# The up projection of a conv FFN with its weights stationary: transposes and copies of u left out

## The chip, the cores and the metric

The program runs on one core of one Trainium2 chip, in one launch. The metric is device microseconds of an execution; the time before is the median of three runs. One more execution was profiled, and the rows below come from that one.

## What is computed

Two transformer blocks, one after the other, on 256 tokens of width 2048, in float32. The change lies in the feed-forward part of the first block:

```
def conv_ffn(h, w_up, w_conv, b_conv, w_down):
    u = h @ w_up                                  # 256 x 2048 by 2048 x 11264
    up = jnp.pad(u, ((0, 0), (CONV_W - 1, 0), (0, 0)))
    conv = b_conv
    for j in range(CONV_W):                       # CONV_W = 3, over the tokens
        conv = conv + w_conv[j] * up[:, j:j + S]
    gate, val = jnp.split(conv, 2, axis=-1)
    return (jax.nn.silu(gate) * val) @ w_down     # 256 x 5632 by 5632 x 2048
```

`h` is the normalised input, with a shift and a scale that come from `c`. The convolution runs along the tokens, with weights of its own for each of the 11264 features.

## The kernel before, in words

Every large product is made of three: each float32 operand is split into a high and a low part (type fp32r), and high x high, high x low and low x high are summed in PSUM. A **unit** is one block of 256 x 512 weights (512 KB): a DMA on SyncE's queue brings it into a `raw` tile (6 buffers), ScalarE casts the high part into an `hl` tile (line 157, 5 buffers), VectorE subtracts for the low part (line 79), and TensorE makes 12 matmuls of it. In between stand jobs that `pump` puts in (`vec_unit`, lines 170 to 175): each loads 512 KB of the modulation weights `w_ada` or `w_mod` into a `raw` tile of the same six and lets VectorE reduce it against `c` in one instruction (L175).

`gemm_gen` (lines 366 to 401) has the activations stationary: `lhsT` is a 128 x 128 piece of `h` (128 features by 128 tokens), the weights move with 512 columns, and the sum stands in PSUM with tokens on the partitions. `up_half` copies it to `u` with ScalarE (L1012), or adds it to `u` with VectorE (L79). The convolution needs the features on the partitions and the tokens along the row, so `conv_half` transposes `u` with TensorE in 8 pieces of 128 x 128 (L1025), into two PSUM tiles `tp`. Then come, for each of 4 groups of 128 features, one ScalarE instruction with bias and the last tap (L1029) and two VectorE instructions for the other taps (L1031, L1033). `glu` multiplies silu(gate) with val and splits the product into `gThi` and `gTlo`.

A **half** is 512 features of gate or of val; a pair `j` of 11 is one half of each. The first four pairs are made in two passes: the first pass (`NH`) makes k = 0 to 7 of their 8 halves (4 units each) while the rest of `h` is still waiting for its scale; the second makes k = 8 to 15 (4 units each). The other 7 pairs have 8 units in each half. The pairs come in four rounds (0 to 2, 3 to 5, 6 to 8, 9 and 10), and each round is followed by its part of the down projection: 4 columns blocks `c`, each of 6 units (4 in the last round), in the order of the pairs; so the units of the round's last pair stand at the end of each block.

Four PSUM tiles `mm` of 2 KB a partition go round; each half and each column block takes two. Program order is not the order on the engines: a scheduler orders the instructions of each engine when the program is built, and each engine then runs its own list in that order. In the list of an engine a waiting instruction holds back all behind it.

Of the kernel before, what the change touches and what calls it, by code (L numbers as in the profile page):

```python
# [13 lines left out]
AF = mybir.ActivationFunctionType  # L14
# [7 lines left out]
KT = 2  # L22
# [7 lines left out]
def block_pair_kernel(ctx: ExitStack, tc: tile.TileContext, T: dict, out: bass.AP):  # L30
# [32 lines left out]
    def ps_mm(name="mm"):  # L63
        n_s4[0] += 1
        return psp.tile([128, 512], F32, name=f"{name}_{n_s4[0]}", tag="mm", bufs=4)
# [98 lines left out]
    def pump(n):  # L164
        for _ in range(n):
            if not jobs:
                return
            jobs.popleft()()
# [101 lines left out]
    def load_split(blk, n, big=False):  # L270

        raw = raw_tile()
        nc.sync.dma_start(raw[:, :KT * n], blk)
        rv = raw[:, :KT * n].rearrange("p (k n) -> p k n", k=KT)
        if big:
            hl = [s4([128, KT, 512], F32R, name="hl")[:, :, :n] for _ in range(2)]
        else:
            n_s4[0] += 1
            t = sp.tile([128, 2, KT, 512], F32R, name=f"hl_{n_s4[0]}", tag="hl", bufs=NHL)
            hl = [t[:, b, :, :n] for b in range(2)]  # L280
        split(hl[0], hl[1], rv)
        return hl
# [719 lines left out]
    gT = {}  # L1002
    us = {}

    def up_half(j, half, k, nk, rate, head=0):
        if (j, half) not in us:
            us[j, half] = s4([128, 2, 512], name="u")
        u = us[j, half]

        def ev(t, p):  # L1010
            if k == 0:
                SC.copy(u[:, t, :], p)  # L1012
            else:
                tt(u[:, t, :], u[:, t, :], p, OP.add)
        gemm(stF, T["w_up"][half * 11 + j], k, nk, ev, rate=rate, head=head)

    def conv_half(j, half):
        u = us.pop((j, half))
        cv = s4([128, 4, 256], name="cv")
        for b in range(2):  # L1020
            p = ps_tp([128, 2, 256])
            for i in range(2):
                for t in range(2):
                    f = b * 2 + i
                    PE.transpose(p[:, i, t * 128:(t + 1) * 128], u[:, t, f * 128:(f + 1) * 128], ident)  # L1025
            for i in range(2):
                f = b * 2 + i
                fi = half * 44 + j * 4 + f
                SC.activation(cv[:, f, :], p[:, i, :], AF.Identity, bias=wcv[:, 3, fi:fi + 1],  # L1029
                              scale=wcv[:, 2, fi:fi + 1])  # L1030
                V.scalar_tensor_tensor(cv[:, f, 1:], p[:, i, :255], wcv[:, 1, fi:fi + 1], cv[:, f, 1:],  # L1031
                                       op0=OP.mult, op1=OP.add)
                V.scalar_tensor_tensor(cv[:, f, 2:], p[:, i, :254], wcv[:, 0, fi:fi + 1], cv[:, f, 2:],  # L1033
                                       op0=OP.mult, op1=OP.add)
        return cv

    def glu(j, cg, cv):
        SC.activation(cg, cg, AF.Silu)
        tt(cv, cg, cv, OP.mult)
        hi = s4([128, 4, 256], F32R, name="gThi")  # L1040
        lo = s4([128, 4, 256], F32R, name="gTlo")
        split(hi, lo, cv)
        gT[j] = (hi, lo)

    def ffn_pair(j, rate):
        k, nk = (8, 8) if j < NH else (0, 16)
        up_half(j, 0, k, nk, rate)
        cg = conv_half(j, 0)
        up_half(j, 1, k, nk, rate)
        glu(j, cg, conv_half(j, 1))  # L1050


    for j in range(NH):
        for half in range(2):
            up_half(j, half, 0, 8, RH, head=HEAD if (j, half) == (0, 0) else 0)
    pump(1000)
    norm_to_pairs(hF, range(4, 8), x1T, rB, A2, SH2)
    job_row("w_ada", 0, 80, COL_BGTF, gtF)
# [247 lines left out]
```

## Time and profile before

| what | us |
|---|---|
| median of 3 runs | 1740.43 |
| lowest, highest | 1739.60, 1742.21 |
| the profiled execution | 1743.09 |
| its span in the trace | 1741.3 |
| TensorE matmul busy | 1692.9 (97%) |
| TensorE weight load busy | 1385.5 (80%) |
| VectorE busy | 1369.1 (79%) |
| ScalarE busy | 910.8 (52%) |

The span is from the first to the last instruction of the program; the 1.8 us around it are start and end. TensorE has two rows: PE is the matmuls, PEld the loads of the stationary operand, which run beside them. Matmuls overlap and their ends are modelled, so 97% busy does not tell how fast they follow each other; that is read from their starts.

### The profile page before, as it was taken

To read this page: it belongs to the slowest core of one execution; us is meant where nothing else is said; L and a number is where in the kernel's file an instruction comes from. 1 tells how busy PE (TensorE), PEld (TensorE's weight loads), DVE (VectorE), ACT (ScalarE), POOL (GpSimd) and SP (SyncE) were. 2 spreads that over 40 slices of the span, in tenths; PEclk is the share of its full clock that TensorE was granted. 3 is DMA by queue.
4 is the path that set the end of the run, shared out by engine and by line. 5 is a ranking of instruction groups with operands and counts; after the bars stand their busy time and mean duration, and the time that the engine had idled before them with its cause. 6 is when DMAs were issued, how large, how long until landed. Compare 5 with 4: busy or idle time off the path is not lost.

```text
span 1741.3 us, 22010 instructions
## 1 busy us (share of the span) xinstructions
PE 1692.9 (97%) x7786; PEld 1385.5 (80%) x7786; DVE 1369.1 (79%) x2079; ACT 910.8 (52%) x1283; POOL 4.2 (0%) x15
## 2 busy tenths in 40 slices
PE   8899999999999989999999999999999999999997
PEld 6688888878778868788888788887888777888886
DVE  8899999998978767599677676777877777766765
ACT  4644354767854456555455544555345565454443
POOL 0000000000000000000000000000000000000000
PEclk9999999999999999999999999999999999999999
DMA  8999988588868868677877787777777748778762
GB/s 324 342 333 324 339 324 278 191 295 295 277 224 323 287 206 313 214 242 238 296 247 251 232 268 261 260 245 261 272 255 252 248 160 269 255 254 277 238 201 94
DMA packets 127495, 455.59 MB, mean 262 GB/s; under 512 B 14357, under 2 KB 15893, under 8 KB 127385
## 3 DMA queue, kind: packets, MB, share of 16 engines
q1 hardware_dynamic: 127384, 454.19, 77.0%
q8 instruction: 61, 1.00, 0.2%
q14 instruction: 50, 0.40, 0.1%
HBM read 452.04 MB, written 2.10 MB: 261 GB/s over the span
## 4 chain that ended last, share of the span: by engine, by line
PE 59%; DMA 18%; DVE 14%; issue 5%; ACT 3%; SPq 0%; DVEq 0%; ACTq 0%
PE mm L378 51%; DMA raw<-in_w_mod 13%; DVE hl L79 5%; DMA raw<-in_w_ada 4%; DVE raw L175 3%; PE keep L378 2%; ACT hl L157 1%; PE mm L1171 1%; DVE cv L1031 1%; PE tp L1025 1%; DVE score L599 1%; DVE cv L1033 0%; DVE pacc L79 0%; PE tp L922 0%; DMA cst<-in_cst 0%
## 5 line engine op out<-in xcount | busy, mean ns | idle before, releaser
L157 ACT CAST hl<-raw 128x1024 fp32r<-128x1024 f32 (+2 forms) x564 | 586.6, 1046 | 584.5 <-PE mm L378 432.0
L79 DVE TENSOR_TENSOR hl<-raw,hl 128x1024 fp32r<-128x1024 f32 (+2 forms) x564 | 675.7, 1212 | 141.5 <-ACT hl L157 140.8
L378 PE MATMUL mm<-hl,hN 128*128 128x512 f32 x2880 | 676.4, 394 | 6.6 <-DVE hN L79 2.4
L378 PEld LDWEIGHTS mm<-hl,hN 128*128 128x128 f32 x2880 | 540.8, 190 | 121.3 <-DVE hN L79 4.0
L175 DVE SCALAR_TENSOR_TENSOR raw<-raw,cB 128x1024 f32<-128x1024 f32 x288 | 350.5, 1220 | 184.7 <-DMA raw<-in_w_mod 139.9
L378 PE MATMUL mm<-hl,hT 128*128 128x512 f32 (+1 forms) x1248 | 290.9, 392 | 8.0 <-ACT hT L157 3.3
L378 PEld LDWEIGHTS mm<-hl,hT 128*128 128x128 f32 x1248 | 234.2, 190 | 56.5 <-ACT hl L157 4.1
L378 PE MATMUL mm<-hl,gThi 128*128 128x512 f32 x704 | 219.9, 395 | 6.2 <-DVE hl L79 3.4
L378 PEld LDWEIGHTS mm<-hl,gThi 128*128 128x128 f32 x704 | 132.9, 190 | 35.9 <-DVE hl L79 5.0
L378 PE MATMUL mm<-hl,gTlo 128*128 128x512 f32 x352 | 137.8, 395 | 0.0
L378 PE MATMUL mm<-hl,pair 128*128 128x512 f32 x384 | 89.5, 392 | 0.0
L378 PE MATMUL mm<-hl,zT 128*128 128x512 f32 x384 | 87.5, 389 | 0.0
L378 PEld LDWEIGHTS mm<-hl,zT 128*128 128x128 f32 x384 | 71.9, 188 | 14.8
L378 PEld LDWEIGHTS mm<-hl,pair 128*128 128x128 f32 x384 | 71.5, 188 | 14.6
L378 PEld LDWEIGHTS mm<-hl,gTlo 128*128 128x128 f32 x352 | 66.9, 190 | 13.8 <-DVE gTlo L79 0.2
L1029 ACT ACTIVATE cv<-tp,wcv 128x256 f32<-128x256 f32 x88 | 44.9, 562 | 47.9 <-DVE cv L1033 39.4
L79 DVE TENSOR_TENSOR pacc<-pacc,mm 128x512 f32<-128x512 f32 (+1 forms) x78 | 52.2, 671 | 6.8 <-PE mm L378 6.3
L378 PE MATMUL mm<-hl,oaT 128*128 128x512 f32 x192 | 48.0, 399 | 0.0
L378 PE MATMUL mm<-hl,obT 128*128 128x512 f32 x192 | 47.1, 397 | 0.6 <-DVE obT L79 0.6
L378 PE MATMUL keep<-hl,hT 128*128 128x512 f32 x192 | 45.7, 395 | 0.8 <-DVE hl L79 0.8
L378 PEld LDWEIGHTS keep<-hl,hT 128*128 128x128 f32 x192 | 36.5, 191 | 9.0 <-DVE hl L79 1.6
L378 PEld LDWEIGHTS mm<-hl,obT 128*128 128x128 f32 x192 | 35.1, 188 | 8.0 <-DVE obT L79 1.0
(331 smaller groups left out, 1191.1 us busy)
## 6 DMA issues: line engine op xcount, KB each, us to landing
raw<-in_w_ada SPq DMA_DIRECT2D x192, 512.0 KB, 4.8
raw<-in_w_up SPq DMA_DIRECT2D x176, 512.0 KB, 4.6
raw<-in_w_in SPq DMA_DIRECT2D x112, 512.0 KB, 5.1
raw<-in_w_mod SPq DMA_DIRECT2D x96, 512.0 KB, 4.5
raw<-in_w_down SPq DMA_DIRECT2D x88, 512.0 KB, 4.6
raw<-in_pool_w_in SPq DMA_DIRECT2D x64, 512.0 KB, 4.5
raw<-in_w_o SPq DMA_DIRECT2D x32, 512.0 KB, 4.9
raw<-in_pool_w_out SPq DMA_DIRECT2D x32, 512.0 KB, 4.3
```

Source lines behind the costliest of these rows:

```text
L79: return V.tensor_tensor(o, a, b, op=op)
L157: SC.copy(hi, src)
L175: V.scalar_tensor_tensor(raw, raw, 1.0, cact[cv][h], op0=OP.mult, op1=OP.mult, accum_out=acc)
L378: PE.matmul(ps[t][:, :n], lhsT=st(k0 + k, t, a), rhs=hl[b][:, i, :], start=(part[0] and k == 0 and x == 0), stop=(part[1] and k == nk - 1 ...
L599: V.scalar_tensor_tensor(score, r[:, i, :], w, score, op0=OP.mult, op1=OP.add)
L1025: PE.transpose(p[:, i, t * 128:(t + 1) * 128], u[:, t, f * 128:(f + 1) * 128], ident)
L1029: SC.activation(cv[:, f, :], p[:, i, :], AF.Identity, bias=wcv[:, 3, fi:fi + 1], scale=wcv[:, 2, fi:fi + 1])
L1031: V.scalar_tensor_tensor(cv[:, f, 1:], p[:, i, :255], wcv[:, 1, fi:fi + 1], cv[:, f, 1:], op0=OP.mult, op1=OP.add)
L1171: PE.matmul(pv[:, q, :], lhsT=hls[k // 2][wa][:, k % 2, f * 128:(f + 1) * 128], rhs=pooled[i][xb][:, k, :], start=(k == 0 and x == 0), sto ...
```

## The change

All halves but the first half of the first pair (in both of its passes) are now made by `up_feat`: for each unit the weights are stationary in 4 pieces of 128 features, and the 256 tokens of `h` move, so that PSUM has the features on the partitions. A unit is 24 matmuls of 256 columns in place of 12 of 512. The four PSUM rows of a half (two tiles, two rows of 256 in each) are held from its first matmul to its last tap. `taps` is the old code of the convolution in a function of its own; it reads the sums from PSUM, or, for the pairs in two passes, from `uT`, to which the second pass is added (`tt`). The copies of `u`, the transposes and the tiles `u` of these halves are gone.

```
+    def up_feat(j, half, k, nk, rate):
+        W = T["w_up"][half * 11 + j]
+        ps = [ps_mm().rearrange("p (q t) -> p q t", q=2) for _ in range(2)]
+        nu = nk // KT
+        for u in range(nu):
+            hl = load_split(W[k // KT + u], 512)
+            for f in range(4):
+                for i in range(KT):
+                    for x, (a, b) in enumerate(((0, 0), (1, 0), (0, 1))):
+                        PE.matmul(ps[f // 2][:, f % 2, :], lhsT=hl[a][:, i, f * 128:(f + 1) * 128],
+                                  rhs=hF[k // 2 + u][:, b, i, :], start=(u == 0 and i == 0 and x == 0 and f % 2 == 0),
+                                  stop=(u == nu - 1 and i == KT - 1 and x == 2), skip_group_check=True)
+            credit[0] += rate
+            while credit[0] >= 1.0:
+                pump(1)
+                credit[0] -= 1.0
+        return ps
+
+    def up_first(j, half, rate):
+        ps = up_feat(j, half, 0, 8, rate)
+        u = us[j, half] = s4([128, 4, 256], name="uT")
+        for b in range(2):
+            SC.copy(u[:, 2 * b:2 * b + 2, :], ps[b])
+
+    def taps(j, half, cv, b, p):
+        for i in range(2):
+            f = b * 2 + i
+            fi = half * 44 + j * 4 + f
+            SC.activation(cv[:, f, :], p[:, i, :], AF.Identity, bias=wcv[:, 3, fi:fi + 1],
+                          scale=wcv[:, 2, fi:fi + 1])
+            V.scalar_tensor_tensor(cv[:, f, 1:], p[:, i, :255], wcv[:, 1, fi:fi + 1], cv[:, f, 1:],
+                                   op0=OP.mult, op1=OP.add)
+            V.scalar_tensor_tensor(cv[:, f, 2:], p[:, i, :254], wcv[:, 0, fi:fi + 1], cv[:, f, 2:],
+                                   op0=OP.mult, op1=OP.add)
+
+    def up_conv(j, half, rate):
+        u = us.pop((j, half), None)
+        ps = up_feat(j, half, 0 if u is None else 8, 16 if u is None else 8, rate)
+        cv = s4([128, 4, 256], name="cv")
+        for b in range(2):
+            p = ps[b]
+            if u is not None:
+                p = u[:, 2 * b:2 * b + 2, :]
+                tt(p, p, ps[b], OP.add)
+            taps(j, half, cv, b, p)
+        return cv
...
     def ffn_pair(j, rate):
-        k, nk = (8, 8) if j < NH else (0, 16)
-        up_half(j, 0, k, nk, rate)
-        cg = conv_half(j, 0)
-        up_half(j, 1, k, nk, rate)
-        glu(j, cg, conv_half(j, 1))
+        if j == 0:
+            up_half(j, 0, 8, 8, rate)
+            cg = conv_half(j, 0)
+        else:
+            cg = up_conv(j, 0, rate)
+        glu(j, cg, up_conv(j, 1, rate))
...
-            up_half(j, half, 0, 8, RH, head=HEAD if (j, half) == (0, 0) else 0)
+            if (j, half) == (0, 0):
+                up_half(j, half, 0, 8, RH, head=HEAD)
+            else:
+                up_first(j, half, RH)
```

How the order on the engines changes is shown at three places. In the names, `hl` is a unit's split weights, `hN` a piece of `h`, `mm` a PSUM sum; L1017, L1040 and L1042 are the matmul and the two VectorE taps of the new code.

TensorE where one full half ends and the next begins, in the third round; before:

```order
L378 MATMUL mm_9610<-hl_9725,hN_6382 128x512 x6
L378 MATMUL mm_9611<-hl_9725,hN_6382 128x512 x6
L378 MATMUL mm_9610<-hl_9742,hN_6383 128x512 x6
L378 MATMUL mm_9611<-hl_9742,hN_6383 128x512 x6
L1025 MATMUL tp_9766<-cst,u_9609 128x128
L1025 MATMUL tp_9777<-cst,u_9609 128x128
L378 MATMUL mm_9789<-hl_9793,hN_5711 128x512 x2
L1025 MATMUL tp_9766<-cst,u_9609 128x128 x3
L1025 MATMUL tp_9777<-cst,u_9609 128x128 x3
L378 MATMUL mm_9789<-hl_9793,hN_5711 128x512 x4
```

and now:

```order
L1017 MATMUL mm_10613<-hN_6718,hl_10797 128x256 x12
L1017 MATMUL mm_10614<-hN_6718,hl_10797 128x256 x12
L1017 MATMUL mm_10613<-hN_6719,hl_10829 128x256 x12
L1017 MATMUL mm_10614<-hN_6719,hl_10829 128x256 x12
L1017 MATMUL mm_10875<-hN_5711,hl_10879 128x256 x12
```

A unit was 12 matmuls of 512 columns and is 24 of 256; the 8 transposes between the halves are gone.

VectorE at the end of the third round, around the taps of the last half of pair 8, from the last L175 ahead of them to the product that makes `gThi`; before:

```order
L175 SCALAR_TENSOR_TENSOR raw_10078,vs_9825<-raw_10078,cB_8187 128x1024
L79 TENSOR_TENSOR hl_10029<-raw_10027,hl_10029 128x1024
L79 TENSOR_TENSOR hl_10046<-raw_10044,hl_10046 128x1024
L1031 SCALAR_TENSOR_TENSOR cv_9939<-tp_9940,wcv,cv_9939 128x255
...
L1033 SCALAR_TENSOR_TENSOR cv_9939<-tp_9951,wcv,cv_9939 128x254
L175 SCALAR_TENSOR_TENSOR raw_10119,vs_9825<-raw_10119,cB_8186 128x1024
L1031 SCALAR_TENSOR_TENSOR cv_9939<-tp_9940,wcv,cv_9939 128x255
...
L1033 SCALAR_TENSOR_TENSOR cv_9939<-tp_9951,wcv,cv_9939 128x254
L79 TENSOR_TENSOR hl_10063<-raw_10061,hl_10063 128x1024
L79 TENSOR_TENSOR cv_9939<-cv_9765,cv_9939 128x1024
```

and now, from the same L175 on (the rows left out are taps):

```order
L175 SCALAR_TENSOR_TENSOR raw_11551,vs_11197<-raw_11551,cB_9025 128x1024
L1040 SCALAR_TENSOR_TENSOR cv_11381<-mm_11137,wcv,cv_11381 128x255
...
L1042 SCALAR_TENSOR_TENSOR cv_11381<-mm_11138,wcv,cv_11381 128x254
L79 TENSOR_TENSOR hl_11478<-raw_11476,hl_11478 128x1024
L1040 SCALAR_TENSOR_TENSOR cv_11381<-mm_11138,wcv,cv_11381 128x255
L79 TENSOR_TENSOR hl_11495<-raw_11493,hl_11495 128x1024
L1042 SCALAR_TENSOR_TENSOR cv_11381<-mm_11138,wcv,cv_11381 128x254
L79 TENSOR_TENSOR hl_11519<-raw_11517,hl_11519 128x1024
L79 TENSOR_TENSOR cv_11381<-cv_11124,cv_11381 128x1024
```

Between the L175 in the middle and the product stood 4 taps and one subtraction of weights; now there stand 6 taps and three subtractions.

VectorE at the end of the last round, around the taps of the last half of pair 10; before, the three subtractions of the column block 0 and 1 ahead of them (`hl_11178` to `hl_11242`) and the first behind them:

```order
L79 TENSOR_TENSOR hl_11178<-raw_11176,hl_11178 128x1024
L175 SCALAR_TENSOR_TENSOR raw_11274,vs_10572<-raw_11274,cB_8187 128x1024
L79 TENSOR_TENSOR hl_11198<-raw_11196,hl_11198 128x1024
L79 TENSOR_TENSOR hl_11242<-raw_11240,hl_11242 128x1024
L1031 SCALAR_TENSOR_TENSOR cv_11106<-tp_11107,wcv,cv_11106 128x255
...
L1033 SCALAR_TENSOR_TENSOR cv_11106<-tp_11118,wcv,cv_11106 128x254
L79 TENSOR_TENSOR hl_11259<-raw_11257,hl_11259 128x1024
```

and now:

```order
L175 SCALAR_TENSOR_TENSOR raw_13038,vs_12099<-raw_13038,cB_9026 128x1024
L79 TENSOR_TENSOR hl_12942<-raw_12940,hl_12942 128x1024
L79 TENSOR_TENSOR hl_12962<-raw_12960,hl_12962 128x1024
L1040 SCALAR_TENSOR_TENSOR cv_12880<-mm_12637,wcv,cv_12880 128x255
...
L1042 SCALAR_TENSOR_TENSOR cv_12880<-mm_12638,wcv,cv_12880 128x254
L79 TENSOR_TENSOR hl_13006<-raw_13004,hl_13006 128x1024
```

The last two subtractions ahead of the taps were unit 3 of column block 0 and unit 0 of block 1 (`hl_11242`); now they are units 2 and 3 of block 0, and unit 0 of block 1 (`hl_13006`) comes behind six of the eight taps.

## Rows read from the trace of the kernel before

**Rows 1.** The page, parts 1 and 4: engines' busy time; the chain that ended last.

```profile
PE 1692.9 (97%) x7786; PEld 1385.5 (80%) x7786; DVE 1369.1 (79%) x2079; ACT 910.8 (52%) x1283; POOL 4.2 (0%) x15
...
PE 59%; DMA 18%; DVE 14%; issue 5%; ACT 3%; SPq 0%; DVEq 0%; ACTq 0%
```

**Rows 2.** Windows: stretch, us, busy PE, PEld, DVE, ACT, POOL, clock, DMA, GB/s.

```profile
1080.00:1120.00 40.00, 40.00 (x184) 32.65 (x184) 28.04 (x42) 21.29 (x27) 0.00 (x0) 1.00 0.80 261
...
1200.00:1240.00 40.00, 37.30 (x161) 30.13 (x160) 32.10 (x42) 17.33 (x20) 0.00 (x0) 0.96 0.83 276
```

**Rows 3.** Groups: matmuls on h, and transposes of u; busy us, mean ns, idle before.

```profile
L378 PE MATMUL mm<-hl,hN 128*128 128x512 f32 x2880 | 676.4, 394 | 6.6 <-DVE hN L79 2.4 <-ACT hN L242 2.4 <-DVE hl L79 1.8
...
L1025 PE MATMUL tp<-cst,u 128*128 128x128 f32 x176 | 27.3, 278 | 0.9 <-DVE u L79 0.9
```

**Rows 4.** Timeline of ScalarE within a full half: start, us, what, [idle before].

```profile
1078.22 1.05 ACT L157 CAST hl<-raw 128x1024 fp32r<-128x1024 f32 x1 [1.67 <-PE mm L378]
1080.94 1.06 ACT L157 CAST hl<-raw 128x1024 fp32r<-128x1024 f32 x1 [1.67 <-PE mm L378]
```

**Rows 5.** Timeline of TensorE in the pool stage, L1171: weights stationary, 256 columns.

```profile
1633.52 0.28 PE L1171 MATMUL mm<-pllo,hl 128*128 128x256 f32 x1
...
1636.40 0.28 PE L1171 MATMUL mm<-pllo,hl 128*128 128x256 f32 x1
1636.52 0.62 PE L1171 MATMUL mm<-plhi,hl 128*128 128x256 f32 x3
```

**Rows 6.** Windows: L1171's matmuls of 256, then 512 columns within a half.

```profile
1626.60:1640.50 13.90, 13.90 (x117) 13.84 (x116) 12.22 (x22) 7.16 (x10) 0.00 (x0) 1.00 0.67 215
1064.50:1078.40 13.90, 13.90 (x63) 11.52 (x62) 8.40 (x11) 5.45 (x6) 0.00 (x0) 1.00 0.80 263
```

**Rows 7.** Timeline of TensorE: transposes after two full halves in a row.

```profile
1086.19 0.38 PE L1025 MATMUL tp<-cst,u 128*128 128x128 f32 x2
...
1109.07 0.38 PE L1025 MATMUL tp<-cst,u 128*128 128x128 f32 x2
```

**Rows 8.** Timeline of TensorE: transposes after halves of 4 units.

```profile
761.89 0.38 PE L1025 MATMUL tp<-cst,u 128*128 128x128 f32 x2
...
773.70 0.38 PE L1025 MATMUL tp<-cst,u 128*128 128x128 f32 x2
...
900.57 0.42 PE L1025 MATMUL tp<-cst,u 128*128 128x128 f32 x2 [0.93 <-DVE u L79]
```

**Rows 9.** Timeline of TensorE: waits for VectorE within the up projection.

```profile
739.67 2.56 PE L378 MATMUL mm<-hl,hN 128*128 128x512 f32 x10 [1.01 <-DVE hN L79]
...
1194.10 1.21 PE L378 MATMUL mm<-hl,hN 128*128 128x512 f32 x4 [1.21 <-DVE hl L79]
...
1356.51 1.20 PE L378 MATMUL mm<-hl,hN 128*128 128x512 f32 x4 [0.61 <-DVE hl L79]
```

**Rows 10.** Timeline of TensorE at the end of the third round.

```profile
1202.21 0.39 PE L1025 MATMUL tp<-cst,u 128*128 128x128 f32 x2
...
1217.07 2.35 PE L378 MATMUL mm<-hl,gThi 128*128 128x512 f32 x6 [2.70 <-ACT gThi L157]
```

**Rows 11.** Timeline of VectorE at the same place.

```profile
1205.29 1.22 DVE L175 SCALAR_TENSOR_TENSOR raw<-raw,cB 128x1024 f32<-128x1024 f32 x1 [3.01 <-DMA raw<-in_w_mod]
...
1208.71 0.86 DVE L1031 SCALAR_TENSOR_TENSOR cv<-tp,wcv,cv 128x255 f32<-128x255 f32 x2
1209.50 0.86 DVE L1033 SCALAR_TENSOR_TENSOR cv<-tp,wcv,cv 128x254 f32<-128x254 f32 x2
1210.82 1.22 DVE L175 SCALAR_TENSOR_TENSOR raw<-raw,cB 128x1024 f32<-128x1024 f32 x1 [0.46 <-DMA raw<-in_w_mod]
...
1213.54 1.21 DVE L79 TENSOR_TENSOR hl<-raw,hl 128x1024 fp32r<-128x1024 f32 x1
1214.67 1.22 DVE L79 TENSOR_TENSOR cv<-cv,cv 128x1024 f32<-128x1024 f32 x1
```

**Rows 12.** Timeline of TensorE at the end of the last round.

```profile
1377.85 0.52 PE L378 MATMUL mm<-hl,gThi 128*128 128x512 f32 x1 [3.37 <-DVE hl L79]
```

**Rows 13.** Timeline at the end of the second round: ScalarE, then TensorE.

```profile
1008.51 1.04 ACT L157 CAST gThi<-cv 128x1024 fp32r<-128x1024 f32 x1
...
1010.02 1.52 PE L378 MATMUL mm<-hl,gThi 128*128 128x512 f32 x6
```

More of the change, by code (lines that the diff above doesn't have):

```diff
@@ L1025, in conv_half @@
                     PE.transpose(p[:, i, t * 128:(t + 1) * 128], u[:, t, f * 128:(f + 1) * 128], ident)
[L1026 to L1034, printed above, removed]
+            taps(j, half, cv, b, p)
         return cv
```

## The prediction

> **What bounds the kernel now.** I read the page first, then the windows over the feed-forward part, then the timelines of TensorE there. The page has TensorE's matmuls busy for 97% of the span, and the chain that ended last runs over PE for 59% of it, then over DMA and VectorE [rows 1]. The windows say where: in a stretch with full halves PE is busy for all 40 us, at full clock, VectorE for 28 and ScalarE for 21 of them [rows 2]. That TensorE sets the pace there is shown by ScalarE: each cast of a unit's weights waits 1.67 us for a matmul to give an `hl` buffer back, and the casts stand 2.72 us apart [rows 4]; that is 12 matmuls of 0.2267 us. The mean of 394 ns in the group [rows 3] is a matmul's length and not its pace, since they overlap. But TensorE does not bound everywhere. At the ends of the third and the last round it waits 2.70 and 3.37 us for `gThi` and for `hl` [rows 10, 12], and the clock in that window falls to a mean of 0.96 [rows 2]. So the change is costed in two parts: TensorE's own stream, and the places where VectorE is late.
>
> **The matmuls, term 1.** All 22 halves have 8 units each, 176; the first half of pair 0 stays as it was, so 168 units change from 12 x 512 to 24 x 256 columns. The kernel has that very form already, in the pool stage: L1171 has weights from `hl` tiles stationary and 256 columns moving. From 1633.52 to 1636.40 stand 24 of its matmuls, 0.120 us each [rows 5]; over a whole stretch the count gives 13.90 us for 117, 0.119 [rows 6]. I take 0.1197, between them. A unit is then 24 x 0.1197 = 2.873 us against 2.720: half as many columns cost more than half, as if 13 ns went to each matmul whatever its size (0.2267 - 0.2133 for 512 columns at 2.4 GHz). The term is 168 x 0.153 = **+25.7 us**; with 0.119 and 0.120 it is +23 and +27. All of it is on the path while TensorE sets the pace.
>
> The Trainium skill, TensorE: Matmul & The Clock Gate, section Back-to-back issue gap, gives a warm gap of N / 2.4 + 2.5 ns, where the trace here has about 13 ns on top of the columns; by the page the term would be an estimated 5 us. The measured pace decides.
>
> **The transposes, term 2.** From one half's first transposes to the next half's 22.88 us pass [rows 7]; 8 units are 8 x 2.72 = 21.76, so 8 transposes with the changes of kind around them cost TensorE 1.12 us. After the halves of 4 units it is 11.81 - 10.88 = 0.93 [rows 8]. The change drops 14 of the first kind and 7 of the second: 15.7 + 6.5. One set also waited 0.93 us for VectorE's sum into `u` [rows 8], and that goes too. **-23.1 us.** So the stream alone is nearly even, +2.6: what the transposes cost, the shorter matmuls take.
>
> **Copies and additions.** ScalarE's copies of `u` go in the 14 halves without a second pass; the other changed halves keep one copy, and their additions on VectorE stay, from PSUM into `uT`. ScalarE has half of its time free [rows 1] and is ahead by a buffer [rows 4]: nothing. If its cover went, ScalarE would have to lose 1.67 us a unit first. The taps stay as many and as long. They now hold the `mm` tiles of their half; the same two tiles are wanted again one half later, some 23 us, and the taps end about 11 us after the half's last matmul (1213.5 against 1202.2 [rows 10, 11]): no wait, except in the last round (term 4).
>
> **Waits that go, term 3.** In the first pass 28 of the 168 units lie ahead of the wait for `hN` at 739.67, so TensorE comes there 4.3 us later; it waited 1.01 [rows 9], and I take that as gone. The waits of 1.21 and 0.61 us [rows 9] stand behind taps that had an L175 in their middle, held by its DMA; half of it is taken off. **-1.9 us**, bounds 0 and -2.8.
>
> **VectorE's order at the ends of the rounds, term 4.** Here the change moves what TensorE waits for. In the third round VectorE reaches the first tap 6.5 us after the half's last matmul (1208.71 against 1202.2 [rows 10, 11]); what holds it is an L175 that waits 3.01 us for its DMA and two subtractions behind it, and these stand ahead of the taps as before. From the L175 in the middle to the product there were 4 taps and 1 subtraction; now there are 6 and 3. A tap takes 0.40 us (two in 0.79) and a subtraction 1.13 [rows 11]: `gThi` comes 0.8 + 2.3 = 3.1 us later. TensorE also has 1.12 us less to do before it wants it, since the transposes that stood there are gone, so term 2 credits here what only lengthens a wait: +4.2. In the last round TensorE had three units of work when the taps began, and has two now: 2.7 more, and again the 1.12: +3.8. At the end of the second round `gThi` was ready at 1009.55 and wanted at 1010.02 [rows 13], 0.47 us of slack; two more subtractions make it 1.8 us late, and the first round has the same pattern: +3.6. Together 11.6. The landing of those DMAs is not fixed, though, and subtractions made earlier need not be made later; the first tap may start up to 1.1 us earlier without the transposes. I take two thirds, **+7.7 us**, between 0 (the order hides behind DMA waits) and 13.
>
> **The sum.** 25.7 - 23.1 - 1.9 + 7.7 = +8.4 us. The profiled execution took 1743.09 us, 1741.3 of span and 1.8 around it; it would take 1751.5. The median of the runs is 2.7 us lower, 1740.43, so the forecast is **1748.8**, slower by 0.5%. A difference of under 0.2%, 3.5 us, is about what this measurement cannot tell from none.
>
> **Rivals.**
> *The stream is even and the ends don't show.* If VectorE's first tap follows the last matmul more closely, or the L175s of the round ends land earlier, term 4 is 0 to 3: the sum is between -0.2 and +3.6, some 1742, no change. For it: VectorE stands idle for DMA just there, 3.01 and 0.46 us [rows 11]. Against it: the extra subtractions stand ahead of the product whatever the DMA does.
> *Faster: taps no longer wait for TensorE.* Before, the taps hung on a copy and on transposes in TensorE's list; now they may begin with the last matmul. If the first tap comes within some 3 us of it rather than 6.5, the waits at the round ends go: 2.70 + 3.37, the other 0.9 of term 3, and the time at the low clock behind the two long waits, some 1.6 us of each 40 us window at a mean of 0.96 [rows 2]. The sum is 25.7 - 23.1 - 2.8 - 6.1 - 3.2 = -9.5, so 1731. It is decided by whether the L175 ahead of the taps still holds VectorE; the order says that it does.
> *The split costs nothing.* If two matmuls of 256 cost what one of 512 costs, term 1 is 0 and the sum -17.3: 1723. That is where the page's gap rule above points; 24 matmuls of L1171 speak against it.
> *Weight loads become the bound.* In L1171's stretch the loads fill 13.84 of 13.90 us, against 11.52 with 512 columns, where one takes 11.52 / 62 = 0.186 us [rows 6]. They overlap each other at 256 columns, or the pace could not be 0.12. If the first load of each unit stood open for want of its `hl`, that would be 168 x 0.066 = +11 on top, 1760; if none overlapped, 168 x (24 x 0.186 - 2.87) = some +270. The Trainium skill, Perfetto Trace Analysis, section Identifying the Most-Contended Engine, would judge TensorE by the busy share of its weight loads and not of its matmuls; by that the up projection would be at its limit after the change. The trace has the pace of 0.12 at that limit already.
>
> **How the numbers follow.** The forecast, slower by 4 to 14 us, has 0.52; no change 0.25; faster by earlier taps 0.11; faster because the split is free 0.02; slower by open weight loads 0.10. That is 0.13 faster, 0.25 same, 0.62 slower. The range takes in the forecast with the bounds of its terms (term 4 at 0 gives 1741.1, at 13 with term 1 at 27 gives 1755.4) and the no-change case down to 1737; open loads add a little above, to 1758. The forecast's own range is 1744 to 1756.
>
> **What would show it.** TensorE's new line should have 24 matmuls in 2.87 us and the casts of ScalarE stand that far apart; halves should follow each other in 23.0 us, against 22.88, with no transposes. The wait for `gThi` at the end of the third round should be about 7 us, at the end of the last round a wait of about the same, and at the ends of the first two some 1.5 where there was none. The wait for `hN` before the second pass should be gone. The prediction is wrong if the pace of the new matmuls is not 0.12, or if TensorE's waits at the round ends are no longer than before; then the time is that of the rivals.

## The result

| | before | after |
|---|---|---|
| median of the runs beside each other (4 and 4) | 1740.01 | 1761.07 |
| lowest, highest | 1739.53, 1742.21 | 1760.36, 1761.75 |
| the profiled execution, its span | 1743.09, 1741.3 | 1760.36, 1758.6 |

The ratio is 1.012 with an interval from 1.0107 to 1.0134: slower by 21 us where 8 were forecast, and above the range. Between the two profiled executions it is 17.3 us, since that of before lay 3.1 above its median and that of after 0.7 below. The page of after, parts 1 and 4, beside [rows 1]:

```profile
PE 1695.7 (96%) x9634; PEld 1473.7 (84%) x9634; DVE 1372.4 (78%) x2079; ACT 896.7 (51%) x1255; POOL 4.2 (0%) x15
...
PE 59%; DMA 17%; DVE 15%; issue 6%; ACT 3%; DVEq 0%; ACTq 0%; SPq 0%
```

TensorE's busy time is 3 us up, the span 17: the loss is waiting. The groups of after for the new matmuls and for ScalarE's activations of the convolution (busy us, mean ns, then idle before them and what ended it):

```profile
L1017 PE MATMUL mm<-hN,hl 128*128 128x256 f32 x4032 | 489.2, 284 | 3.0 <-DVE hl L79 3.0
L1038 ACT ACTIVATE cv<-mm,wcv 128x256 f32<-128x256 f32 x56 | 31.4, 565 | 94.2 <-DVE cv L1042 77.3 <-PE mm L1017 16.8
```

ScalarE now waits 77.3 us in 19 places ahead of its activations for VectorE's taps (L1042). The stream of a full half is as forecast; ScalarE's casts, which stood 2.72 us apart [rows 4], and the windows beside [rows 2] (stretch, us, busy PE, PEld, DVE, ACT, POOL, clock, DMA, GB/s):

```profile
1079.78 1.05 ACT L157 CAST hl<-raw 128x1024 fp32r<-128x1024 f32 x1 [1.83 <-PE mm L1017]
1082.66 1.05 ACT L157 CAST hl<-raw 128x1024 fp32r<-128x1024 f32 x1 [1.83 <-PE mm L1017]
```

```profile
1080.00:1120.00 40.00, 39.80 (x331) 39.59 (x331) 22.73 (x30) 16.06 (x19) 0.00 (x0) 1.00 0.68 226
1200.00:1240.00 40.00, 31.14 (x170) 26.76 (x169) 28.16 (x39) 16.86 (x19) 0.00 (x0) 0.91 0.75 246
```

A unit takes 2.88 us. The end of the third round is where TensorE loses most. Its timeline there, to be read beside [rows 10]; then at the end of the last round, beside [rows 12]:

```profile
1210.34 0.63 PE L378 MATMUL mm<-hl,gThi 128*128 128x512 f32 x2
...
1221.72 0.39 PE L378 MATMUL mm<-hl,gTlo 128*128 128x512 f32 x1
1230.57 2.07 PE L378 MATMUL mm<-hl,gThi 128*128 128x512 f32 x4 [8.46 <-ACT gThi L157]
...
1390.52 0.76 PE L378 MATMUL mm<-hl,gThi 128*128 128x512 f32 x1 [5.95 <-DVE cv L1042]
1391.95 0.79 PE L378 MATMUL mm<-hl,gThi 128*128 128x512 f32 x1 [0.67 <-DVE hl L79]
```

The down projection begins at 1210.34 and has work without the last pair for 11.4 us, until 1221.72; then `gThi` is missing for 8.5 us. VectorE at the same place, beside [rows 11]:

```profile
1214.17 1.23 DVE L175 SCALAR_TENSOR_TENSOR raw<-raw,cB 128x1024 f32<-128x1024 f32 x1 [3.74 <-DMA raw<-in_w_mod]
...
1215.33 2.36 DVE L79 TENSOR_TENSOR hl<-raw,hl 128x1024 fp32r<-128x1024 f32 x2
1217.60 0.48 DVE L1040 SCALAR_TENSOR_TENSOR cv<-mm,wcv,cv 128x255 f32<-128x255 f32 x1
1218.11 0.48 DVE L1042 SCALAR_TENSOR_TENSOR cv<-mm,wcv,cv 128x254 f32<-128x254 f32 x1
1221.27 1.23 DVE L175 SCALAR_TENSOR_TENSOR raw<-raw,cB 128x1024 f32<-128x1024 f32 x1 [2.67 <-DMA raw<-in_w_mod]
...
1223.98 1.21 DVE L79 TENSOR_TENSOR hl<-raw,hl 128x1024 fp32r<-128x1024 f32 x1
1225.12 0.47 DVE L1040 SCALAR_TENSOR_TENSOR cv<-mm,wcv,cv 128x255 f32<-128x255 f32 x1
1225.51 1.21 DVE L79 TENSOR_TENSOR hl<-raw,hl 128x1024 fp32r<-128x1024 f32 x1
1226.64 0.47 DVE L1042 SCALAR_TENSOR_TENSOR cv<-mm,wcv,cv 128x254 f32<-128x254 f32 x1
1227.03 1.21 DVE L79 TENSOR_TENSOR hl<-raw,hl 128x1024 fp32r<-128x1024 f32 x1
1228.17 1.22 DVE L79 TENSOR_TENSOR cv<-cv,cv 128x1024 f32<-128x1024 f32 x1
```

The product (last row) starts 17.95 us after the half's last matmul; before it was 12.69. Two taps stand ahead of the L175 in the middle where four did, that L175 waits 2.67 us where it waited 0.46, and three subtractions stand between it and the product where one did.

Within the halves of that round TensorE now waits four times for `hl`:

```profile
1114.62 6.02 PE L1017 MATMUL mm<-hN,hl 128*128 128x256 f32 x48 [0.20 <-DVE hl L79]
1121.58 14.65 PE L1017 MATMUL mm<-hN,hl 128*128 128x256 f32 x120 [0.93 <-DVE hl L79]
1136.85 5.42 PE L1017 MATMUL mm<-hN,hl 128*128 128x256 f32 x43 [0.63 <-DVE hl L79]
...
1175.80 0.39 PE L1017 MATMUL mm<-hN,hl 128*128 128x256 f32 x1 [1.25 <-DVE hl L79]
```

ScalarE (first fence) stands 8.69 us ahead of the second activation of a PSUM tile until VectorE's taps of the first are done, and the casts of the next weights stand behind it in its list. But TensorE does not wait for these casts. The wait at 1121.58 ends with the first subtraction of 1120.30, and its weights were the last of the four that ScalarE cast from 1106.25 to 1110.12. On VectorE (second fence) this subtraction stands behind an L175 that waited 3.45 us for `w_mod`:

```profile
1106.25 3.87 ACT L157 CAST hl<-raw 128x1024 fp32r<-128x1024 f32 x4
...
1123.60 0.56 ACT L1038 ACTIVATE cv<-mm,wcv 128x256 f32<-128x256 f32 x1 [8.69 <-DVE cv L1042]
1124.07 1.04 ACT L157 CAST hl<-raw 128x1024 fp32r<-128x1024 f32 x1
```

```profile
1112.20 1.23 DVE L175 SCALAR_TENSOR_TENSOR raw<-raw,cB 128x1024 f32<-128x1024 f32 x1 [3.66 <-DMA raw<-in_w_mod]
...
1113.35 2.35 DVE L79 TENSOR_TENSOR hl<-raw,hl 128x1024 fp32r<-128x1024 f32 x2
1119.15 1.22 DVE L175 SCALAR_TENSOR_TENSOR raw<-raw,cB 128x1024 f32<-128x1024 f32 x1 [3.45 <-DMA raw<-in_w_mod]
...
1120.30 2.36 DVE L79 TENSOR_TENSOR hl<-raw,hl 128x1024 fp32r<-128x1024 f32 x2
```

It is so at all four places: the cast was done 2.7 to 10.2 us before the subtraction began, and a few instructions ahead of the subtraction an L175 had waited 1.36 to 3.66 us. Of the round's 48 units none was cast less than 1.8 us before TensorE began it. VectorE itself waited for casts for 3.0 us there, in three places; that much ScalarE's standing may have put into it. What is smaller is VectorE's **lead**, the time from the end of a unit's subtraction to the unit's first matmul: its median over the round's 48 units is 5.0 us before and 2.0 after.

By rounds, from the first matmul of one to the first of the next (up and down projection; round 1 with the first pass), worked out from the starts in the traces. The columns "product" are the product's start at the ends of rounds 3 and 4, in us behind the half's last matmul; "waits" is what TensorE waits for `hl` within the halves of round 3, and "lead" is VectorE's median lead there. The rows e1 to e10 are the experiments below, each from its profiled execution:

| | round 1 | round 2 | round 3 | round 4 | product, 3 | product, 4 | waits, 3 | lead, 3 |
|---|---|---|---|---|---|---|---|---|
| before | 229.6 | 188.1 | 208.8 | 150.3 | 12.7 | 13.4 | 1.2 | 5.0 |
| after | 229.2 | 190.7 | 218.7 | 154.6 | 17.95 | 16.0 | 3.0 | 2.0 |
| e1 | 230.0 | 188.4 | 218.1 | 155.4 | 15.7 | 14.0 | 3.5 | 2.4 |
| e2 | 230.4 | 188.3 | 206.3 | 148.3 | 9.4 | 9.7 | 0 | 4.6 |
| e3 | 230.3 | 189.7 | 205.2 | 174.5 | 9.4 | 10.1 | 0 | 8.6 |
| e4 (before) | 228.8 | 199.4 | 203.6 | 172.6 | 10.3 | 8.6 | 0 | 7.8 |
| e5 | 229.2 | 188.3 | 213.7 | 149.1 | 12.3 | 11.1 | 3.3 | 2.3 |
| e6 | 236.2 | 186.8 | 213.7 | 152.6 | 16.3 | 14.1 | 0 | 5.6 |
| e7 (before) | 230.2 | 191.0 | 205.0 | 149.0 | 11.5 | 12.9 | 0 | 7.1 |
| e8 | 232.9 | 188.3 | 205.1 | 145.3 | 8.2 | 7.5 | 0 | 4.8 |
| e9 (before) | 229.5 | 193.8 | 202.6 | 144.0 | 9.3 | 9.3 | 0 | 6.2 |
| e10 | 230.3 | 188.3 | 213.7 | 150.0 | 9.8 | 9.5 | 3.4 | 4.5 |

Of the 17.3 us, 9.9 come in round 3, 4.4 in round 4, 2.6 in round 2. In round 3, 4.3 arise within the halves and 5.6 in the down projection behind them.

### The profile page after: what moved, and what is told of

It is laid out like the page before. It is cut to its first block, busy times and chain, and to the rows that moved or that the text cites. A ratio compares the mean times of both kernels' runs of the same rounds, so it can differ in the third digit from the quotient of the medians.

```text
span 1758.6 us, 25669 instructions
## 1 busy us (share of the span) xinstructions
PE 1695.7 (96%) x9634; PEld 1473.7 (84%) x9634; DVE 1372.4 (78%) x2079; ACT 896.7 (51%) x1255; POOL 4.2 (0%) x15
## 4 chain that ended last, share of the span: by engine, by line
PE 59%; DMA 17%; DVE 15%; issue 6%; ACT 3%; DVEq 0%; ACTq 0%; SPq 0%
PE mm L378 39%; PE mm L1017 13%; DMA raw<-in_w_mod 13%; DVE hl L79 6%; DVE raw L175 3%; PE keep L378 2%; DMA raw<-in_w_ada 2%; ACT hl L157 1%; PE mm L1220 1%; DVE cv L1040 1%; DVE cv L1042 1%; DVE score L599 0%; DVE pacc L79 0%; DMA raw<-in_w_pb 0%; DVE xsq L79 0%
## 5 line engine op out<-in xcount | busy, mean ns | idle before, releaser
L79 DVE TENSOR_TENSOR hl<-raw,hl 128x1024 fp32r<-128x1024 f32 (+2 forms) x564 | 677.9, 1213 | 156.4 <-ACT hl L157 155.4
L175 DVE SCALAR_TENSOR_TENSOR raw<-raw,cB 128x1024 f32<-128x1024 f32 x288 | 350.8, 1221 | 184.0 <-DMA raw<-in_w_mod 141.9
L1017 PE MATMUL mm<-hN,hl 128*128 128x256 f32 x4032 | 489.2, 284 | 3.0 <-DVE hl L79 3.0
L1017 PEld LDWEIGHTS mm<-hN,hl 128*128 128x128 f32 x4032 | 487.6, 193 | 5.3 <-DVE hl L79 3.8
L378 PE MATMUL mm<-hl,gThi 128*128 128x512 f32 x704 | 221.5, 397 | 17.5 <-ACT gThi L157 10.3
L378 PE MATMUL mm<-hl,hN 128*128 128x512 f32 x864 | 203.1, 394 | 4.6 <-ACT hN L242 2.4
L378 PEld LDWEIGHTS mm<-hl,hN 128*128 128x128 f32 x864 | 161.6, 189 | 39.9 <-DVE hN L79 3.5
L378 PEld LDWEIGHTS mm<-hl,gThi 128*128 128x128 f32 x704 | 133.6, 191 | 48.2 <-ACT gThi L157 11.1
L1038 ACT ACTIVATE cv<-mm,wcv 128x256 f32<-128x256 f32 x56 | 31.4, 565 | 94.2 <-DVE cv L1042 77.3
```

What stands on the lines that cost most here:

```text
L79: return V.tensor_tensor(o, a, b, op=op)
L175: V.scalar_tensor_tensor(raw, raw, 1.0, cact[cv][h], op0=OP.mult, op1=OP.mult, accum_out=acc)
L378: PE.matmul(ps[t][:, :n], lhsT=st(k0 + k, t, a), rhs=hl[b][:, i, :], start=(part[0] and k == 0 and x == 0), stop=(part[1] and k == nk - 1 ...
L1017: PE.matmul(ps[f // 2][:, f % 2, :], lhsT=hl[a][:, i, f * 128:(f + 1) * 128], rhs=hF[k // 2 + u][:, b, i, :], start=(u == 0 and i == 0 and ...
```

## The experiments

Three theories. **T1**: VectorE's own list is at fault; an L175 that waits for its DMA stands between the last taps. **T2**: ScalarE and VectorE take turns at a PSUM tile, ScalarE stands still and the casts behind it come late. **T3**: the ring of six `raw` buffers is too short, so that VectorE waits for a DMA which itself waited for VectorE. The medians below stand beside runs of the kernel before on the same chip (1743.82 for e1 to e4, 1740.52 for e5 to e8, 1739.17 for e9 and e10); across groups the ratios compare.

**e1**, the sums copied to SBUF again, in `up_conv`:

```diff
+            else:
+                if b == 0:
+                    v = s4([128, 4, 256], name="uT")
+                p = v[:, 2 * b:2 * b + 2, :]
+                SC.copy(p, ps[b])
             taps(j, half, cv, b, p)
```

> The changed kernel, except that ScalarE again copies the sums of the one-pass halves to SBUF and the taps and activations read that copy; the transposes stay away. T1 (VectorE's own list: subtractions hl and products L175 that wait for their DMA stand between the taps) expects about the time of the kernel after, 1757 to 1764 us, with gThi at the end of round 3 still 7 to 9 us late, since VectorE's list hardly changes. T2 (the activations of ScalarE and the taps of VectorE read the same PSUM tile in turn, and ScalarE stands still meanwhile with the weight casts behind it) expects most of what the last pairs of the rounds lost (+4.3 +5.6 +3.7 of the stages, with the cold clock after them) to come back: 1744 to 1752 us, the wait at the end of round 3 back to about 3 to 5 us.

1758.32 us, ratio 1.0081 (1.0053 to 1.011): two thirds of the loss stay, and in the rounds of the profiled execution nearly all of it. ScalarE's waits for the taps in front of these activations are gone, so T2, as worded, falls as the sole cause. VectorE at the end of round 3:

```profile
1214.71 1.23 DVE L175 SCALAR_TENSOR_TENSOR raw<-raw,cB 128x1024 f32<-128x1024 f32 x1 [3.78 <-DMA raw<-in_w_mod]
...
1222.10 1.23 DVE L175 SCALAR_TENSOR_TENSOR raw<-raw,cB 128x1024 f32<-128x1024 f32 x1 [2.58 <-DMA raw<-in_w_mod]
...
1226.36 1.22 DVE L79 TENSOR_TENSOR cv<-cv,cv 128x1024 f32<-128x1024 f32 x1
```

The product comes 2.2 us earlier than in after, which is two subtractions fewer ahead of it; the L175 still waits 2.58.

**e2**, both activations of a tile ahead of its taps, in `taps`:

```diff
             SC.activation(cv[:, f, :], p[:, i, :], AF.Identity, bias=wcv[:, 3, fi:fi + 1],
                           scale=wcv[:, 2, fi:fi + 1])
+        for i in range(2):
+            f = b * 2 + i
+            fi = half * 44 + j * 4 + f
             V.scalar_tensor_tensor(cv[:, f, 1:], p[:, i, :255], wcv[:, 1, fi:fi + 1], cv[:, f, 1:],
```

> The changed kernel with both activations of a PSUM tile ahead of its four taps. The taps still read PSUM, but ScalarE does its two activations of a tile without waiting for taps between them. T2 expects ScalarE's waits for taps (50.3 us in ten places from 1068 to 1230) to go almost wholly, and the time at 1744 to 1752 us. T1 expects 1757 to 1764 us. If reading PSUM itself were what makes the taps dear (a rival to both), e2 would stay near the kernel after while e1 came down.

1737.24 us, ratio 0.9956 (0.9937 to 0.9975): below T2's range, and faster than before. But the edit did two things. ScalarE's waits for taps ahead of these activations went (it now stands at silu(gate) instead, up to 7.1 us, with no harm to TensorE in the halves), and VectorE's list changed: in after an L175 stands between the taps of four of the six halves of round 3, here of none, and at the end of the round the L175 of the middle moved behind the product:

```profile
1203.88 1.23 DVE L175 SCALAR_TENSOR_TENSOR raw<-raw,cB 128x1024 f32<-128x1024 f32 x1 [3.85 <-DMA raw<-in_w_mod]
...
1207.31 0.48 DVE L1043 SCALAR_TENSOR_TENSOR cv<-mm,wcv,cv 128x255 f32<-128x255 f32 x1
...
1211.30 0.48 DVE L1045 SCALAR_TENSOR_TENSOR cv<-mm,wcv,cv 128x254 f32<-128x254 f32 x1
1211.70 1.22 DVE L79 TENSOR_TENSOR hl<-raw,hl 128x1024 fp32r<-128x1024 f32 x1
1212.83 1.22 DVE L79 TENSOR_TENSOR cv<-cv,cv 128x1024 f32<-128x1024 f32 x1
```

From the first tap to the product 5.5 us, against 10.6 in after. The taps read PSUM as in after and take the same 0.48 us, so reading PSUM is not dear in itself.

**e3 and e4**, no modulation work handed out in each round's last pair, in the kernels after and before:

```diff
-            ffn_pair(j, FR)
+            ffn_pair(j, FR if j < j1 - 1 else 0)
```

> The changed kernel with no modulation work handed out in the last pair of each round, so that no L175 is put among its taps (the work moves to other pairs). T1 expects the wait for gThi at the end of round 3 to fall from 8.85 us to 3 or less, and the one of the last round likewise: with the cold stretch behind them 10 to 16 us, 1745 to 1751 us. T2 expects less, 3 to 6 us (1755 to 1758), as ScalarE's serial order stays.

> The kernel before with the same edit as e3. It tells what the modulation work in the last pairs cost already there: the waits there were 2.70 and 3.37 us, so T1 expects 3 to 6 us off, 1734 to 1737 us; T2 expects no more than 2 us off. If e3 gains no more than this one, then the edit has nothing to do with what the change lost.

1767.36 (1.0131; 1.0099 to 1.0163) and 1769.36 (1.0144; 1.0109 to 1.0179): both slower, and neither total answers the question. What is not handed out earlier the program hands out in one go in the last round's down projection (27 L175s there, 3 in after), and there TensorE stood, in e3:

```profile
1413.79 1.22 PE L378 MATMUL mm<-hl,gThi 128*128 128x512 f32 x2 [16.72 <-ACT hl L157]
```

The third round by itself tells more: 205.2 us where after has 218.7, with the product 9.4 us behind the matmuls. Activations and taps take turns there as in after. But the round has less work as well, 24 L175s where after has 32, and one of them still stands between the last taps and waits 1.84 us.

**e5**, the same number of jobs, those of the round's last half handed out behind its product (`late` is true for a round's last pair, and `rate1` is then 0, else `rate`; a half has 8 steps, or 4 in the pairs of two passes):

```diff
-        glu(j, cg, up_conv(j, 1, rate))
+        glu(j, cg, up_conv(j, 1, rate1))
+        if late:
+            credit[0] += rate * (2 if j < NH else 4) * 2
+            while credit[0] >= 1.0:
+                pump(1)
+                credit[0] -= 1.0
```

> The changed kernel, with the modulation jobs of the last half of each round handed out behind that half's product instead of within it; no job is left out or moved to another round. In VectorE's list the L175 that stood between the taps at the end of rounds 2 to 4 then stands behind the product, or ahead of the first tap; the activations and taps still read PSUM in turn. T1 (an L175 between the taps, waiting for its DMA) expects the waits at the end of round 3 (8.85 us) and of the last round (6.34 and 1.43) to fall to about 2 us each and the cold stretches behind them to go: 1744 to 1750 us. T2 (ScalarE and VectorE take turns at a PSUM tile) expects 1756 to 1762 us.

1746.5 us, ratio 1.004 (1.0023 to 1.0057), in T1's range: some 14 us of the 21 are back with PSUM read as in after. In VectorE's list at the end of round 3 the L175 of the middle now stands between the last tap and the product and waits for nothing. What is left is mostly in round 3, whose halves still take 142.2 us (before 137.6). The jobs of its other halves stand as in after: an L175 is between the taps of four of the six, and TensorE waits 3.3 us for subtractions that stand behind an L175.

**e6 and e7**, seven `raw` buffers, in the kernels after and before:

```diff
-    NS4, NRAW, NHL = 28, 6, 5
+    NS4, NRAW, NHL = 27, 7, 5
```

> The changed kernel with seven buffers raw in place of six (and 27 in place of 28 of the tag s4, for room). T3 (the ring of buffers that SP loads into: a load of in_w_mod is issued only when VectorE has freed a buffer, so VectorE waits for a DMA that waited for VectorE) expects VectorE's waits of L175 for in_w_mod (45.3 us in 19 from 1068 to 1230) to fall by half and the time to 1742 to 1752 us. T1 alone gives the same sign by less, since the order of the list changes too. If the DMA queue itself is what is late, the waits stay, and the time stays at 1757 to 1763 us.

> The kernel before with the same seven buffers, as the control of e6. T3 expects 1732 to 1738 us (the waits of 2.70 and 3.37 us at the ends of rounds go, with a few of the waits inside). If e6 gains clearly more than e7, the change had made the ring's shortness dearer; if both gain alike, the ring has nothing to do with what the change lost.

1756.61 (1.0104; 1.0078 to 1.013) and 1741.54 (1.0002; 0.9985 to 1.0018). By its own marks T3 falls, at least for one more buffer: the time is above its range, and VectorE's waits for `w_mod` in the feed-forward part (us, times, longest) are in after and in e6:

```profile
DVE raw L175 <- DMA raw<-in_w_mod: 95.9, 43, 4.4
```

```profile
DVE raw L175 <- DMA raw<-in_w_mod: 95.7, 48, 4.6
```

But the total hides what the ring does. In rounds 2 to 4 e6 is 11.0 us faster than after, and e7 2.2 faster than before. In e6 the halves of round 3 take 138.1 us as in e8, TensorE has no wait in them and VectorE's lead is 5.6 us, though activations and taps take turns as in after. Round 1 is 7.0 us longer, and there TensorE waits for `hN` (us, times, longest):

```profile
PE mm L378 <- DVE hN L79: 5.1, 2, 4.2
```

Whether that wait comes from the seventh buffer or from the `s4` buffer that it took the place of, no run shows. In VectorE's list, too, an L175 stands between the taps of two of the six halves where four had one. So the short ring, or the list that the scheduler makes with it, has a share in the loss within the halves; the late product at the end of round 3 (16.3 us) stays.

**e8**, the edits of e2 and e5 together:

> The edits of e2 and e5 together. In e2 no L175 stood between the last taps any more, so T1 expects little on top of it: 1733 to 1739 us, within 4 us of e2. T2 expects the same as e2. More than 4 us below e2 would mean that the L175 ahead of the taps matters by itself.

1736.7 us, ratio 0.9977 (0.9961 to 0.9992): by the ratios 0.2% above e2, with intervals that overlap, and 10 us below e5 in the same group. So the edit of e2 is still worth 10 us: 4.1 within the halves of round 3 (138.1 against 142.2 us), the rest at the ends of rounds 3 and 4, where the product comes 4.1 and 3.6 us earlier. In round 3 the first tap starts 2.7 us behind the last matmul, in e5 5.3; 1.1 more is the L175 ahead of e5's product. That does not part T1 from T2, for e5 had cleared the last halves alone: an L175 stands between the taps of four of the six halves of round 3 in e5, and of one in e8.

**e9**, the kernel before with no L175 between the last taps. The jobs of a round's last pair go to the pair ahead and behind the product (`rate`, `rate1`, `late` per step):

```diff
-            ffn_pair(j, FR)
+            ffn_pair(j, *((0, 0, 0.6) if j == j1 - 1 else (0.6, 0.6, 0) if j == j1 - 2 else (FR, FR, 0)))
```

> The kernel before, with the modulation jobs of the last two pairs of each round handed out elsewhere (0.6 per step in the second last pair, none in the last, the rest behind its product), so that in VectorE's list no L175 stands between the last taps, as in e2, e5 and e8. It prices the kernel before without the stall that e2 and e8 had taken out of the kernel after. T1 expects the waits of about 3 us at the ends of round 3 and of the last round to go with what the clock loses behind them: 1731 to 1736 us. Then the kernels before and after differ by less than 4 us once neither has the stall (e8 was 1736.7 us), which is what the matmuls, the transposes and the waits that went sum to (+0.7 us). If it stays at 1739 to 1742 us, e8's gain on the kernel before is from elsewhere.

1735.31 us, ratio 0.9972 (0.9959 to 0.9986), as T1 expected. The gain of 4 to 5 us is what is left of two effects: by the profiled executions rounds 3 and 4 are 6.2 and 6.3 us shorter, and round 2 is 5.7 longer. TensorE waits 3.5 us there for VectorE's sum into `u`, which stands behind an L175 that waited 4.29 us. All of TensorE's waits of this kind in the four rounds (us, times, longest; before one of 0.9):

```profile
PE tp L1025 <- DVE u L79: 4.6, 2, 3.5
```

So the jobs among the last taps of rounds 3 and 4 cost some 12 us already before the change. The totals of e8 and e9 are level, 0.9977 and 0.9972, but partly by chance: e9 carries its 5.7 us in round 2, and e8's round 1 is 3.3 us longer than that of before.

**e10**, the edits of e1 and e5 together:

> The edits of e1 (copies to SBUF, so no taking turns at the PSUM tile) and e5 (no L175 between the last taps) together. The sum of two causes expects what e8 gave, or a little more for the copies on ScalarE: 1736 to 1742 us, with the product at the end of round 3 starting 8 to 10 us behind the last matmul of the up projection (before 12.7, after 17.95, e1 15.7, e5 12.3). If reading PSUM had a price of its own in the taps, it would come out below e8; if e1's copies cost ScalarE what they save VectorE, at 1745 us or more, with e5.

1748.22 us, ratio 1.0048 (1.0029 to 1.0067): above what was expected, level with e5. The product comes early as expected (9.8 us), yet round 3 takes 213.7. In the midst of it TensorE waits 3.17 us for `hl`, until 1127.62. ScalarE had cast these weights 12.3 us before VectorE subtracted; in VectorE's list an L175 stood between the taps, and four taps behind it, ahead of the subtraction (ScalarE, then VectorE):

```profile
1113.02 1.05 ACT L157 CAST hl<-raw 128x1024 fp32r<-128x1024 f32 x1
```

```profile
1123.62 1.22 DVE L175 SCALAR_TENSOR_TENSOR raw<-raw,cB 128x1024 f32<-128x1024 f32 x1 [2.17 <-DMA raw<-in_w_mod]
...
1126.35 1.22 DVE L79 TENSOR_TENSOR hl<-raw,hl 128x1024 fp32r<-128x1024 f32 x1
```

ScalarE stands still here too, 9.13 us ahead of the cast of `gThi`, but only after this cast. So T1 holds in wider words: an L175 that waits for its DMA holds back the subtractions and taps behind it, within the halves as at the ends of the rounds. T2 as worded is not borne out: in none of TensorE's waits for `hl` within the halves of round 3, in after, e1, e5 or e10, was ScalarE's cast late.

## Why the prediction was wrong

The direction was as forecast; the time lay 3 us above the range. The terms one by one:

- **Term 1** held. The new matmuls start 0.120 us apart, 2.88 us a unit, as L1171's did. The Trainium skill's rule of N / 2.4 + 2.5 ns for matmuls by themselves (TensorE: Matmul & The Clock Gate, Back-to-back issue gap) would be an estimated 0.109; the trace, where each matmul has a weight load, does not agree. Weight loads fill 39.59 of 40 us and add nothing to that pace: the rival of open loads is out, and so is that of a free split. That the measured 1761 lies next to the 1760 of open loads is chance; by that rival a unit would take 2.94 us.
- **Term 2** held with it. With the stall out of both (e9 and e8), rounds 3 and 4 take 202.6 and 144.0 us before and 205.1 and 145.3 after; in e8 TensorE still waits 1.2 us in round 3 and 0.4 in round 4. So the stream is 1.2 and 0.9 us longer, where 48 and 32 units of +0.153 less 6 and 4 sets of 1.12 give +0.6 and +0.4.
- **Term 3** failed in part: the wait for `hN` inside the second pass went (and so did the one for `u`, counted in term 2). But the two waits for `hl` of [rows 9], 1.8 us, of which half was taken off, gave way to four others of 3.0 us. The prediction had put them down to an L175 that is held by its DMA, and so are the four.

**Term 4 failed, by its size.** It was worked out at 11.6 and cut to 7.7, for "the landing of those DMAs is not fixed". TensorE's waits behind the last matmuls of the rounds grew by 11.2 us: from 0 to 1.8 in round 2, from 2.7 to 8.9 in round 3, from 3.4 to 6.6 in the last; round 1, where 1.8 was put, has none. So the cut was wrong. That the working comes near in sum is partly luck: round 1 makes up for round 3, where 4.2 was put and 6.2 came. What was left out in round 3 is the landing, which is not free to fall either way: SP issues the next load of `w_mod` when VectorE gives a buffer back. SP's issues in before, then in after:

```profile
1206.55 0.33 SPq L173 DMA_DIRECT2D raw<-in_w_mod  x1
```

```profile
1216.57 0.33 SPq L173 DMA_DIRECT2D raw<-in_w_mod  x1
```

In before that is as the L175 ahead of the taps ends (1206.51); in after it is 1.2 us past the end of that L175 (1215.41), with the first subtraction behind it. So the wait of the L175 in the middle grew by 2.2 us: 1.2 by the later issue, and 0.8 by the two taps that had covered it and now stand behind it. I priced the taps and the subtractions, 3.1 us, and let the wait be; the product came 5.3 us later.

In sum, the rounds are 16.5 us longer. TensorE's waits make 10.8 of it, where terms 2 to 4 had 4.9. The stream makes some 4.7 (168 units of +0.16 less the transposes' 22.2), where 3.5 stood. The rest, about 1 us, is not parted.

**A wait that was passed over** stands under "Copies and additions": the activations and the taps both read the `mm` tiles, and ScalarE lost 8.69 us at once between them. It was there to be seen: in before ScalarE's activations of the convolution waited 39.4 us in 14 places for taps, on the `tp` tiles, but with both activations of a tile in a row. The Trainium skill has the rule (PSUM — Partial Sum Buffer, PSUM bank collisions raise a hardware error): two engines may not access one bank in the same partitions at once, reads included, so software must order them. By it activations and taps on an `mm` tile had to go in turn; the trace agrees, with the 77.3 us of waits above. That this standing cost TensorE anything beyond the 3.0 us that VectorE waited for casts is not shown: no cast of round 3 came late, and e3 and e6 have the same turns and none of these waits. The edit of e2, with what it moves in the lists, is worth the 10 us between e5 and e8.

Of the marks that were named beforehand the pace and the 23.0 us between halves came true; the wait at the end of round 3 was 8.5 us and not 7; at the last round it was 5.95 for an `mm` tile that the taps still held and 0.67 for `hl`, against 3.37 for `hl` before; at the end of round 2 `gThi` is 1.8 us late; at the end of round 1 there is nothing.

What is left open: how much of the 10 us between e5 and e8 is ScalarE's standing, and how much VectorE's list, which the scheduler made anew in e8; no run parts them, and the traces speak for the list. Why VectorE's lead fell from 5.0 to 2.0 us with the change is open too; the edit of e2 and a seventh `raw` buffer each bring it back. More than seven were not tried.

## What to carry to other kernels

Where a change is nearly even on the engine that bounds (here 27 us more of matmuls, some 22 less of transposes), the result is decided by where the schedule then puts the other engines' instructions: read each list at the places where the bounding engine runs dry, and price a waiting instruction with what covers its wait, not by its length. When a change makes two engines read one PSUM tile, try the order of the readers: both activations ahead of the taps turned +1.2% into −0.4% here, by way of VectorE's list as far as the traces show. When an engine waits, ask whether what it waits for was late, or only stood behind another wait in the list of the engine that makes it: ScalarE's long waits were the most striking rows here, and the casts behind them were in time. Work put in as filler should not be handed out in the last stretch before a dependency, but it must go somewhere: e3 paid 17 us for leaving it over.

## What the runs showed that was not expected

What the clock cost did not follow the length of the wait alone. The windows behind the waits at the end of round 3 and of the last round, in before (waits of 2.7 and 3.4 us) and in after (8.5, and 6.0 with 0.7 behind it):

```profile
1217.00:1220.00 3.00, 2.93 (x8) 2.30 (x9) 3.00 (x4) 0.97 (x2) 0.00 (x0) 0.63 0.74 251
1378.00:1382.00 4.00, 4.00 (x11) 3.16 (x12) 4.00 (x4) 1.04 (x1) 0.00 (x0) 0.57 0.64 189
```

```profile
1230.60:1234.60 4.00, 4.00 (x10) 3.18 (x11) 3.45 (x4) 0.86 (x1) 0.00 (x0) 0.55 0.81 275
1234.60:1240.00 5.40, 5.40 (x25) 4.46 (x25) 3.61 (x6) 2.11 (x2) 0.00 (x0) 1.00 0.78 252
1392.00:1398.00 6.00, 6.00 (x14) 4.74 (x15) 5.22 (x7) 0.83 (x2) 0.00 (x0) 0.50 0.76 212
```

The clock is at the lower of its two levels, 1.2 GHz, for most of these few us and then back at 2.4. Matmuls of 512 columns then start 0.427 us apart and not 0.227. At the end of round 3 seven do so in before and seven in after, 1.4 us each time, though the wait is three times as long; at the end of the last round seven and thirteen, 1.4 and 2.6 us.

Weight loads that fill 99% of a stretch, where they had filled 82%, did not make the pace slower than L1171's 0.120 us. A unit costs 6% more; whether the shorter matmuls or the loads set that pace, no run shows.
